# A decoder step bound by TensorE: the high and low parts of the activations start at 44 different pairs of places in 256-byte blocks, and one ring's low weights stand 192 bytes beyond the high ones instead of 64

## The chip, the cores and the metric

One core of a Trainium2 chip runs the whole program as one launch. The metric is device time in microseconds (us). The median of two runs of the kernel before is 2691.72 us (2691.7 and 2691.73).

## What is computed

A two-layer decoder step on 320 tokens (256 of a prompt and 64 of 8 sample sequences), model width 2048, all in float32:

```
layer 0: gated linear attention (w_in: 2048 x 6144, w_out: 2048 x 2048), norm, MLP, norm
layer 1: gMLP spatial gating   (w_in: 2048 x 4096, w_out: 2048 x 2048), norm, MLP, norm
MLP:     square(relu(x @ w1)) @ w2          w1: 2048 x 8192, w2: 8192 x 2048
norm:    layer_norm(alpha * x + sublayer(x))
```

Nearly all the arithmetic is in products of a 2048 x 2048 block of weights with the 320 tokens. There are 23 such blocks: three of the attention's w_in, one of its w_out, four of w1 and four of w2 in each MLP, two of the gMLP's w_in and one of its w_out.

## The kernel before, in words

Activations lie transposed: features on the 128 partitions, the 320 tokens along the free dimension, and 16 tiles `k` of 128 features after each other. Each float32 operand is split into a rounded part ("high", `fp32r`) and the rest ("low"). A product of the two is three matmuls, in `mm3`: low weights with high activations (L161), high weights with low activations (L162), high weights with high activations (L163). Each loads its own 128 x 128 weights and streams the 320 columns of one activation tile. In what follows, three such matmuls are called a **triplet**.

`gemm` goes over the output columns in groups of 256. `group` goes over four **quarters** `q` of the 16 feature tiles. For each quarter `unit` fetches a 128 x 4 x 256 block of raw weights (512 KB), ACT rounds it into `wh` (L144), DVE subtracts to make `wl` (L145), and TensorE runs 2 x 4 triplets with it: 24 matmuls. So a block of weights is 8 groups x 4 quarters x 8 triplets = 256 triplets, and the quarter changes every 8 triplets.

The split weights go into rings of four buffers for high and four for low. Ring "a" serves the whole program. Ring "b" is added in `second_half`, during the attention's `w_out`, and from there on units take ring a and ring b in turn. A group has an even number of units, so a given quarter always meets the same ring. `Ring.part` puts a gap of `LINE // 4` = 16 floats (64 bytes) between the high and the low buffers.

Where the tiles start, counted in bytes from the last multiple of 256 (a **place**):

| tile | place before |
|---|---|
| `wh`, both rings | 0 |
| `wl`, both rings | 64 |
| activations `x`, `o`, `y`, `h` (high and low), every feature tile | 128 |
| activations `dg` (see below), feature tile `k` | 8k (0 to 120) |

The feature tiles of width 320 are 1280 bytes apart, five times 256, so all of a tensor have one place. `bigtile` sets it with `start = LINE // 2`. The tensors `dg` are the unnormalised input of the first two groups of a product that follows a norm (`gemm_of`, three times in the program); they have two more columns (322), so their feature tiles are 1288 bytes apart and the place moves by 8 bytes from one to the next. This is called the **raw stage** below.

The pairs of tensors that the change touches are those made by `parts(out, "y")` in `gemm_of` and by `parts(h_in, "h")` in `mlp`. `y` is the normalised input of w1 (and of the gMLP's w_in, and in place of it later the input of the gMLP's w_out); `h` is the input of w2, made afresh for each of the eight w2 blocks.

Of the kernel before, what the change touches and what calls it, by code (L numbers as in the profile page):

```python
# [8 lines left out]
F32 = mybir.dt.float32  # L9
F32R = mybir.dt.float32r  # L10
# [5 lines left out]
P = 128  # L16
# [4 lines left out]
T = TP + DB * DS  # L21
# [9 lines left out]
UK = 4  # L31
UN = 256
NU = KT // UK
WARM = 9
LINE = 64
BIG = KT * T + LINE
# [8 lines left out]
class Ring:  # L45


    def __init__(self, pool, tag):
        self.pool, self.tag, self.gap = pool, tag, False

    def part(self, p, name):

        t = self.pool.tile([P, UK, UN], F32R, tag=p + self.tag, name=name)
        if not self.gap:
            self.pool.tile([P, LINE // 4], F32, tag="gap", name=name + "_gap", bufs=1)
            self.gap = True
        return t


class Side:  # L60
# [17 lines left out]
def step_kernel(ctx: ExitStack, tc: tile.TileContext, A):  # L78
# [3 lines left out]
    def nm(s):  # L82
        uid[0] += 1
        return f"{s}_{uid[0]}"
# [3 lines left out]
    big = ctx.enter_context(tc.tile_pool(name="big", bufs=1))  # L88
# [8 lines left out]
    turn = [0]  # L97
    banks = [0]
    units = [0]

    def mmtile(n=T):

        if mx is not None:
            banks[0] = (banks[0] + 1) % 6
        return (mx if banks[0] > 3 else mm).tile([P, n], F32, tag="mm", name=nm("mm"), padded_shape=[P, 512])
# [19 lines left out]
    def col(c):  # L125
        return vec[:, c : c + 1]
# [38 lines left out]
    def group(w, row0, cols, rh, rl, evict, side=None, width=T, before=None):  # L165

        ps = [mmtile(width) for _ in range(2 * len(cols))]
        for q in range(NU):
            if before is not None:
                before(q)  # L170
            for i, c in enumerate(cols):
                wh, wl = unit(w, row0, q, c, next_ring())
                for n in range(2):
                    for kk in range(UK):
                        k = q * UK + kk
                        mm3(ps[2 * i + n][:], wh, wl, kk, n, rh, rl, k, 0, width, k == 0, k == KT - 1)
                if side is not None:
                    side()
        for n in range(2 * len(cols)):
            evict(n, ps[n])  # L180
# [11 lines left out]
    lp = l2 = z = None  # L192
# [5 lines left out]
    def bigtile(tag, dt, name, width=T):  # L198

        t = (lp if tag == "b1" else big).tile([P, BIG], dt, tag=tag, name=nm(name))
        start = LINE // 2 if width == T else 0
        return t[:, start : start + KT * width].rearrange("p (k t) -> p k t", t=width)

    def parts(pair, name, width=T):
        return bigtile(pair + "0", F32R, name + "h", width), bigtile(pair + "1", F32R, name + "l", width)

    xh, xl = parts("a", "x")  # L210
    o_all = bigtile("b0", F32, "o_all")

    gst = ExitStack()
# [129 lines left out]
    class Head:  # L343


        def __init__(hd, h):
            hd.h = h
            hd.eb, hd.ei, hd.ee = {}, {}, {}
# [484 lines left out]
    def gemm(w, row0, col0, rh, rl, evict, quad=False, side=None, before=None, before_last=None):  # L833

        i = 0
        while i < D // UN:
            n2 = 2 if quad and i == 0 else 1
            group(w, row0, [col0 + (i + m) * UN for m in range(n2)], rh, rl,
                  lambda n, ps, i=i: evict(2 * i + n, ps), side, before=before if i == 0 else before_last if i == D // UN - 1 else None)
            i += n2  # L840

    def gemm_of(norm, out, w, col0, evict_raw, evict):

        yh, yl = parts(out, "y")
        norm.close()
        side = Side([lambda j=j: norm.apply(j, yh, yl) for j in range(KT)], 3 * NU)
        group(w, 0, (col0, col0 + UN), *norm.raw, evict_raw, side, width=TW)
        side.flush()
        for i in range(2, D // UN):
            group(w, 0, (col0 + i * UN,), yh, yl, lambda n, ps, i=i: evict(2 * i + n, ps))  # L850
        return yh, yl

    def residual_gemm(w, rh, rl, row0, scale, vg, vb, raw, quad=False, side=None, before=None, last=False):

        norm = None

        def evict(j, ps):
            nonlocal norm
            if j == 0:
                norm = Norm(z, vg, vb, raw, last)  # L860
            zj = z[:, j, :]
            if j < KT // 2:
                nc.vector.scalar_tensor_tensor(zj, zj, scale, ps[:], op0=ALU.mult, op1=ALU.add)
            else:
                nc.vector.tensor_add(zj, zj, ps[:])
            norm.add(j)
            if j == KT // 2 - 1:
                for i in range(KT // 2, KT):
                    zi = z[:, i, :]
                    nc.vector.scalar_tensor_tensor(zi, zi, scale, norm.c[:], op0=ALU.mult, op1=ALU.subtract)  # L870

        gemm(w, row0, 0, rh, rl, evict, quad, side, before)
        return norm

    def mlp(i, norm, y_in, h_in, vg, vb, raw, last=False):

        w1, w2 = A["mlp_w1"][i], A["mlp_w2"][i]
        NC_ = 4
        for c in range(NC_):
            hs = []  # L880

            def sq_relu(j, x, r):
                if not hs:
                    hs.extend(parts(h_in, "h"))
                hh, hl = hs
                f = l2.tile([P, T], F32, tag="f", name=nm("f"))
                nc.vector.scalar_tensor_tensor(f[:], x, 0.0, r[:], op0=ALU.max, op1=ALU.mult)
                nc.scalar.copy(hh[:, j, 0:T], f[:])
                nc.vector.tensor_sub(hl[:, j, 0:T], f[:], hh[:, j, 0:T].bitcast(F32))

            def evict(j, ps):
                r = l2.tile([P, T], F32, tag="r", name=nm("r"))
                nc.scalar.activation(r[:], ps[:], AF.Relu)
                sq_relu(j, ps[:], r)

            def evict_raw(j, ps):
                t, wb_ = norm.correct(ps)
                r = l2.tile([P, T], F32, tag="r", name=nm("r"))
                nc.scalar.activation(r[:], t[:], AF.Relu, bias=wb_)
                sq_relu(j, r[:], r)  # L900

            if c == 0:
                yh, yl = gemm_of(norm, y_in, w1, 0, evict_raw, evict)
            else:
                gemm(w1, 0, c * D, yh, yl, evict)
            if c < NC_ - 1:
                def evz(j, ps, s=ALPHA if c == 0 else 1.0):
                    nc.vector.scalar_tensor_tensor(z[:, j, :], z[:, j, :], s, ps[:], op0=ALU.mult, op1=ALU.add)
                gemm(w2, c * D, 0, *hs, evz)
            else:  # L910
                return residual_gemm(w2, *hs, c * D, 1.0, vg, vb, raw, last=last)
# [35 lines left out]
    def put_v(j, x, bias):  # L947
        nonlocal v, nv
        if j == 0:
            v = bigtile("a0", F32, "v")  # L950
            nv = Norm(v, V_SG, V_SBB)
        vj = v[:, j, 0:T]
        nc.scalar.activation(vj, x, AF.Gelu, bias=bias)
        if j >= KT // 2:
            nc.vector.tensor_sub(vj, vj, nv.c[:])
        nv.add(j)
        if j == 3:
            spatial()

    def ev_v_raw(j, ps):  # L960
# [3 lines left out]
        put_v(j, t[:], bias[:])  # L964

    yh, yl = gemm_of(norm, "b", A["sg_w_in"], D, ev_v_raw, lambda j, ps: put_v(j, ps[:], col(V_SB + KT + j)))

    nv.close()
# [105 lines left out]
    for j in range(KT):  # L1074
        y, g, b = z[:, j, :], col(norm.vg + j), col(norm.vb + j)
# [78 lines left out]
```

## Time and profile before

| | |
|---|---|
| median of the runs | 2691.72 us |
| the profiled execution: first to last instruction | 2689.4 us |
| around it (median less span) | 2.3 us |
| TensorE (PE) busy | 2680.7 us, 100% of the span |
| weight loads (PEld) busy | 2658.8 us, 99% |
| DVE, ACT busy | 1550.3 us (58%), 1162.5 us (43%) |
| granted TensorE clock | 1.000 |

The profiled execution's time by the runs' measure is its span and the 2.3 us around it. "PE" rows are matmuls and "PEld" rows weight loads, which run beside them. Matmuls are pipelined: the time of one in a row (some 300 ns) is from its start to its modelled end, while the next starts after about 145 ns. What counts for the time is the distance from one start to the next, called the **pitch** below, which a timeline shows, or a row that gives the first start, the last start and the number of matmuls between.

### The profile page before, as it was taken

Reading aid. Unit: us, or ns where it says so; the run is one execution under the profiler, and the core shown is the slowest. Engines: PE = TensorE matmul, PEld = TensorE weight load, DVE = VectorE, ACT = ScalarE, POOL = GpSimd, SP = SyncE. Lnnn points to the kernel's source line nnn. Section 1 sums busy time; section 2 is a strip of 40 time slices with the busy share of each in tenths; the row PEclk is TensorE's granted clock in tenths of the full one; section 3 lists DMA queues with packets and bytes.
Section 4 is the critical chain, followed back from the end, with each engine's and each line's share of the span. In section 5 each row is a group of like instructions: output and inputs, shape, how many; then the busy total and the mean of one; then the engine's idle time right before and its main releaser. Section 6 shows DMA issues by size and latency. Waiting matters only on the chain.

```text
span 2689.4 us, 44906 instructions
## 1 busy us (share of the span) xinstructions
PE 2680.7 (100%) x18395; PEld 2658.8 (99%) x18395; DVE 1550.3 (58%) x2322; ACT 1162.5 (43%) x1638; POOL 226.4 (8%) x391
## 2 busy tenths in 40 slices
PE   9999999999999999999999999999999999999999
PEld 9999999999999999999999999999999999999998
DVE  7677677885444444444478776686444444444446
ACT  5455455564334334333446554355334333333434
POOL 4353341000000000000001032000000000000000
PEclk9999999999999999999999999999999999999999
DMA  8667667545445545444445555455445444454552
GB/s 252 220 196 249 217 198 253 189 142 159 155 150 155 151 150 156 150 153 152 150 152 161 157 158 149 134 165 153 153 150 156 150 152 154 150 155 150 152 154 79
DMA packets 138494, 442.42 MB, mean 165 GB/s; under 512 B 20912, under 2 KB 27952, under 8 KB 138288
## 3 DMA queue, kind: packets, MB, share of 16 engines
q1 hardware_dynamic: 121440, 408.08, 49.2%
q0 software_dynamic: 16304, 30.82, 3.7%
q8 instruction: 144, 2.36, 0.4%
q10 hardware_dynamic: 544, 0.66, 0.1%
q14 instruction: 62, 0.51, 0.1%
HBM read 409.60 MB, written 22.02 MB: 160 GB/s over the span
## 4 chain that ended last, share of the span: by engine, by line
PE 99%; DMA 0%; ACT 0%; DVE 0%; ACTq 0%; issue 0%; DVEq 0%
PE mm L161 32%; PE mm L163 32%; PE mm L162 31%; PE gl L631 1%; PE gl L634 1%; PE gl L589 1%; PE gl L1003 0%; PE gl L573 0%; DMA raw<-gla_w_in 0%; ACT z L1087 0%; DMA xr<-xT 0%; PE gl L558 0%; PE gl L603 0%; PE gl L574 0%; PE gl L552 0%; PE gl L1004 0%
## 5 line engine op out<-in xcount | busy, mean ns | idle before, releaser
L145 DVE TENSOR_TENSOR wl<-raw,wh 128x1024 fp32r<-128x1024 f32 (+1 forms) x740 | 902.3, 1220 | 953.2 <-ACT wh L144 950.9
L144 ACT CAST wh<-raw 128x1024 fp32r<-128x1024 f32 (+1 forms) x740 | 771.5, 1044 | 1251.9 <-PE mm L163 1127.1
L163 PE MATMUL mm<-yh,wh 128*128 128x320 f32 x2624 | 805.9, 307 | 0.0
L161 PE MATMUL mm<-yh,wl 128*128 128x320 f32 x2624 | 803.2, 309 | 0.0
L162 PE MATMUL mm<-yl,wh 128*128 128x320 f32 x2624 | 794.9, 303 | 0.0
L161 PE MATMUL mm<-hh,wl 128*128 128x320 f32 x2048 | 631.5, 308 | 0.0
L163 PE MATMUL mm<-hh,wh 128*128 128x320 f32 x2048 | 629.0, 307 | 0.0
L162 PE MATMUL mm<-hl,wh 128*128 128x320 f32 x2048 | 619.9, 303 | 0.0
L162 PEld LDWEIGHTS mm<-yl,wh 128*128 128x128 f32 x2624 | 492.7, 188 | 0.0
L163 PEld LDWEIGHTS mm<-yh,wh 128*128 128x128 f32 x2624 | 491.4, 187 | 0.0
L161 PEld LDWEIGHTS mm<-yh,wl 128*128 128x128 f32 x2624 | 491.0, 188 | 0.0
L161 PEld LDWEIGHTS mm<-hh,wl 128*128 128x128 f32 x2048 | 384.6, 188 | 0.0
L162 PEld LDWEIGHTS mm<-hl,wh 128*128 128x128 f32 x2048 | 384.6, 188 | 0.0
L163 PEld LDWEIGHTS mm<-hh,wh 128*128 128x128 f32 x2048 | 383.4, 187 | 0.0
L161 PE MATMUL mm<-xh,wl 128*128 128x320 f32 x768 | 238.2, 311 | 1.4 <-DVE wl L145 0.7
L163 PE MATMUL mm<-xh,wh 128*128 128x320 f32 x768 | 236.4, 309 | 0.0
L162 PE MATMUL mm<-xl,wh 128*128 128x320 f32 x768 | 235.2, 306 | 0.0
L161 PEld LDWEIGHTS mm<-xh,wl 128*128 128x128 f32 x768 | 144.1, 188 | 5.4 <-DVE wl L145 1.0
L162 PEld LDWEIGHTS mm<-xl,wh 128*128 128x128 f32 x768 | 144.3, 188 | 4.4 <-issue 1.2
L163 PEld LDWEIGHTS mm<-xh,wh 128*128 128x128 f32 x768 | 143.7, 187 | 2.6 <-issue 0.7
L1053 POOL CAST ident_r<-ident 128x128 fp32r<-128x128 f32 x1 | 0.3, 286 | 1027.9 <-PE gl L772 1027.9
L936 POOL DMA_DIRECT2D bsp<-sg_wT x1 | 0.6, 558 | 999.7 <-PE mm L163 999.7
(265 smaller groups left out, 2380.3 us busy)
## 6 DMA issues: line engine op xcount, KB each, us to landing
raw<-mlp_w SPq DMA_DIRECT2D x512, 512.0 KB, 3.5
raw<-gla_w_in SPq DMA_DIRECT2D x94, 512.0 KB, 4.1
raw<-sg_w_in SPq DMA_DIRECT2D x64, 512.0 KB, 3.6
st<-state SPq DMA_DIRECT2D x32, 512.0 KB, 5.7
o_state_s<-st POOLq DMA_DIRECT2D x32, 512.0 KB, 4.2
raw<-gla_w_out SPq DMA_DIRECT2D x32, 512.0 KB, 4.5
raw<-sg_w_out SPq DMA_DIRECT2D x32, 512.0 KB, 3.5
va<-blk POOLq DMA_DIRECT2D x128, 32.0 KB, 4.3
```

The source lines that it names most:

```text
L144: nc.scalar.copy(hi[:, ks, :], raw[:, ks, :])
L145: nc.vector.tensor_sub(lo[:, ks, :], raw[:, ks, :], hi[:, ks, :].bitcast(F32))
L161: nc.tensor.matmul(ps, wl[:, kk, s], x_h, start=first, stop=False)
L162: nc.tensor.matmul(ps, wh[:, kk, s], x_l, start=False, stop=False)
L163: nc.tensor.matmul(ps, wh[:, kk, s], x_h, start=False, stop=last)
L589: nc.tensor.matmul(pairs(pu), hd.ktp[:, kt, blk, :], hd.v_prompt(blk), start=(blk == 0), stop=(blk == 1))
L631: nc.tensor.matmul(po[:], qm[:, kt, b * P : (b + 1) * P], part[:], start=False, stop=(b == DB - 1 and kt == 1 and part is sth))
L634: nc.tensor.matmul(pairs(pu), kz[:, i, kt, g, :], hd.v_sample(g), start=True, stop=True)
L936: nc.gpsimd.dma_start(wsT, A["sg_wT"])
L1053: nc.gpsimd.tensor_copy(ident_r[:], ident[:])
```

## The change

A class `Act` takes the place of the plain tile for `y` and `h`. It puts each quarter (four feature tiles) at a place of its own, a multiple of 32 bytes given by a table, for the high and the low tensor apart. The quarters stand in the tile in the order of their places, so that they don't overlap; the tile has 256 bytes to spare, as before. The three `y` pairs and the eight `h` pairs with four quarters each make 44 pairs of places (high, low), all different; the pair (4, 4), which is the old 128 and 128, isn't among them. In ring b the gap between high and low weights becomes `3 * LINE // 4` = 48 floats, so its `wl` stands at place 192 instead of 64. Ring a stays.

```
 class Ring:
         self.pool, self.tag, self.gap = pool, tag, False
+        self.apart = LINE // 4 if tag == "a" else 3 * LINE // 4
...
-            self.pool.tile([P, LINE // 4], F32, tag="gap", name=name + "_gap", bufs=1)
+            self.pool.tile([P, self.apart], F32, tag="gap", name=name + "_gap", bufs=1)
...
+class Act:
+    def __init__(self, tile, places):
+        order = sorted(range(NU), key=lambda q: places[q])
+        self.tile = tile
+        self.start = [order.index(q) * UK * T + LINE // 8 * places[q] for q in range(NU)]
+
+    def __getitem__(self, at):
+        p, k, c = at
+        s = self.start[k // UK] + k % UK * T
+        return self.tile[p, s + (c.start or 0) : s + c.stop]
+
+H_PLACES = [
+    ((1, 4, 0, 5), (4, 1, 4, 4)), ((4, 6, 2, 3), (0, 4, 4, 4)), ...
+]
+Y_PLACES = [((4, 1, 6, 0), (7, 3, 0, 7)), ((4, 1, 7, 5), (5, 2, 7, 3)), ((1, 6, 3, 0), (6, 6, 3, 6))]
...
+    def placed(pair, name, places):
+        tiles = []
+        for i in range(2):
+            pool = lp if pair + str(i) == "b1" else big
+            tiles.append(Act(pool.tile([P, BIG], F32R, tag=pair + str(i), name=nm(name + "hl"[i])), places[i]))
+        return tiles
...
-        yh, yl = parts(out, "y")
+        yh, yl = placed(out, "y", Y_PLACES[gemms[0]])
...
-                    hs.extend(parts(h_in, "h"))
+                    hs.extend(placed(h_in, "h", H_PLACES[4 * i + c]))
```

In the built program every engine has the same instructions as before, in the same order and with the same waits; every tile has the same size and buffer. What differs is the address at which `y`, `h` and ring b's `wl` are written and read.

More of the change, by code (lines that the diff above doesn't have):

```diff
@@ L54, in part @@
         if not self.gap:
-            self.pool.tile([P, LINE // 4], F32, tag="gap", name=name + "_gap", bufs=1)
+            self.pool.tile([P, self.apart], F32, tag="gap", name=name + "_gap", bufs=1)
             self.gap = True
         return t
+class Act:
[8 more added lines that the diff above has]
+H_PLACES = [
+    ((1, 4, 0, 5), (4, 1, 4, 4)), ((4, 6, 2, 3), (0, 4, 4, 4)), ((1, 0, 4, 7), (0, 0, 2, 4)), ((1, 1, 5, 2), (1, 5, 1, 0)),
+    ((5, 5, 0, 3), (5, 0, 5, 1)), ((3, 2, 6, 7), (5, 6, 2, 3)), ((4, 4, 6, 7), (3, 6, 5, 0)), ((1, 0, 2, 3), (7, 3, 2, 7)),
+]
+Y_PLACES = [((4, 1, 6, 0), (7, 3, 0, 7)), ((4, 1, 7, 5), (5, 2, 7, 3)), ((1, 6, 3, 0), (6, 6, 3, 6))]
 class Side:
@@ L99, in step_kernel @@
     units = [0]
+    gemms = [0]
     def mmtile(n=T):
@@ L842, in gemm_of @@
     def gemm_of(norm, out, w, col0, evict_raw, evict):
-        yh, yl = parts(out, "y")
+        yh, yl = placed(out, "y", Y_PLACES[gemms[0]])
+        gemms[0] += 1
         norm.close()
```

## The prediction

> **What bounds the kernel now.** I read the page's busy times first, then its chain that ended last, then the groups of matmuls.
>
> ```profile
> span 2689.4 us, 44906 instructions
> ...
> PE 2680.7 (100%) x18395; PEld 2658.8 (99%) x18395; DVE 1550.3 (58%) x2322; ACT 1162.5 (43%) x1638; POOL 226.4 (8%) x391
> ...
> PE 99%; DMA 0%; ACT 0%; DVE 0%; ACTq 0%; issue 0%; DVEq 0%
> ...
> L145 DVE TENSOR_TENSOR wl<-raw,wh 128x1024 fp32r<-128x1024 f32 (+1 forms) x740 | 902.3, 1220 | 953.2 <-ACT wh L144 950.9
> L163 PE MATMUL mm<-yh,wh 128*128 128x320 f32 x2624 | 805.9, 307 | 0.0
> L161 PE MATMUL mm<-yh,wl 128*128 128x320 f32 x2624 | 803.2, 309 | 0.0
> L162 PE MATMUL mm<-yl,wh 128*128 128x320 f32 x2624 | 794.9, 303 | 0.0
> L161 PE MATMUL mm<-hh,wl 128*128 128x320 f32 x2048 | 631.5, 308 | 0.0
> L163 PE MATMUL mm<-hh,wh 128*128 128x320 f32 x2048 | 629.0, 307 | 0.0
> L162 PE MATMUL mm<-hl,wh 128*128 128x320 f32 x2048 | 619.9, 303 | 0.0
> ```
>
> PE is never idle: the chain is 99% PE, and the idle time before the matmuls of `y` and `h` is 0.0. So the kernel's time is the number of matmuls times their pitch, and nothing but the pitch can move it. The last six rows say how many triplets read the moved tensors: 2624 with `y` and 2048 with `h`, together **4672**. One nanosecond more in each triplet is 4.7 us of the kernel.
>
> Now the pitch. The row of L161 in a stretch of 100 us gives the first start, the last start and the count.
>
> ```profile
> L161 PE MATMUL mm<-yh,wl x232: 307/308/309, 999.8 to 1099.9; 128*128 128x320 f32 x116
> ```
>
> There are 231 triplets in 100.1 us: **433.3 ns** for a triplet, all with activations at place 128, high weights at 0 and low weights at 64. All the 100 us are alike: the durations lie within 307 to 309.
>
> Is this pitch a property of the matmuls, or can the places move it? Two things in the trace speak to that. The first is a timeline of the attention stage, behind another kind of matmul (L634), at the same places:
>
> ```profile
> 238.76 0.40 PE L634 MATMUL gl<-va,kz 128*128 128x512 f32 x1
> 239.00 0.31 PE L161 MATMUL mm<-xh,wl 128*128 128x320 f32 x1
> 239.15 0.31 PE L162 MATMUL mm<-xl,wh 128*128 128x320 f32 x1
> 239.29 0.31 PE L163 MATMUL mm<-xh,wh 128*128 128x320 f32 x1
> 239.44 0.31 PE L161 MATMUL mm<-xh,wl 128*128 128x320 f32 x1
> ...
> 239.88 0.31 PE L161 MATMUL mm<-xh,wl 128*128 128x320 f32 x1
> ...
> 241.61 0.31 PE L161 MATMUL mm<-xh,wl 128*128 128x320 f32 x1
> ```
>
> The first triplet takes 440 ns (239.00 to 239.44), the second 440, and the next four together 1.73 us, 432.5 each. The matmuls are the same, the addresses have the same places; only what ran before differs. So a disturbed sequence is some 7 ns slower per triplet, and it settles after two. The second is the raw stage, whose places differ from one feature tile to the next:
>
> ```profile
> 545.16 0.30 PE L161 MATMUL mm<-dgh,wl 128*128 128x322 f32 x1
> ...
> 552.24 0.31 PE L161 MATMUL mm<-dgh,wl 128*128 128x322 f32 x1
> ...
> L161 PE MATMUL mm<-dgh,wl x17: 304/309/315, 545.2 to 552.2; 128*128 128x322 f32 x17
> ```
>
> ```profile
> 559.89 0.31 PE L161 MATMUL mm<-dgh,wl 128*128 128x322 f32 x1
> ...
> 574.12 0.31 PE L161 MATMUL mm<-yh,wl 128*128 128x320 f32 x1
> ...
> L161 PE MATMUL mm<-dgh,wl x32: 308/310/317, 559.9 to 573.7; 128*128 128x322 f32 x32
> ```
>
> These are 16 triplets in 7.08 us (442.5 ns, places 0 to 24) and 32 in 14.23 us (444.7 ns, places 64 to 120), 444.0 on average. Two columns of 322 are extra: at 433.3 / 960 = 0.45 ns a column they cost 2.7 ns a triplet. What is left, 441.3, is **8.0 ns above** the settled triplet at place 128, and the durations spread over 304 to 317 where they were 307 to 309. The trace thus has two levels: 433.3 where places stay and the sequence has settled, about 441 where it is disturbed or the places change.
>
> **The change part by part.**
>
> *The places of `y` and `h`.* No instruction is added or removed, so the term is 4672 triplets times a difference of pitch. The trace has no settled stretch at another place, so I bound it. In the changed kernel the place is constant for the 8 triplets of a unit, and then the next quarter has another.
>
> - Lower bound of the likely cases: every pair settles to the same 433.3, but it has to settle anew in each unit. By the timeline that is two triplets of eight at about +7: 2 / 8 x 7 = 1.75 ns per triplet, or 4672 x 1.75 = 8 us.
> - Upper bound of the likely cases: the new pairs never do better than the raw stage, +8.0 ns on every triplet, or 4672 x 8.0 = 37 us.
>
> The rows nearest to the new stage lie on both sides: like the raw stage it goes through many places, like `y` and `h` before it stays long enough at one to settle. I take the middle, (1.75 + 8.0) / 2 = 4.9 ns a triplet, **+23 us**.
>
> *Ring b's low weights at 192.* This touches every unit of ring b from the attention's `w_out` on, half of the units. Inside `y` and `h` it is one more place among those that the bounds above cover, and I add nothing. Outside, in the raw stage (192 triplets) and most of `w_out`'s 256, at most half of the 448 triplets meet ring b. At the 8 ns of the raw stage either way that is 224 x 8.0 = 1.8 us up or down; I take nothing, since the raw stage's rows show no side.
>
> *The writers.* ACT and DVE write `y`, `h` and `wl` at other addresses. I cost this at nothing, because PE hides it:
>
> ```profile
> ACT wh L144 <- PE mm L163: 1127.1, 514, 3.8
> DVE wl L145 <- ACT wh L144: 950.9, 564, 4.2
> ```
>
> ACT waits 1127 us in all for PE to free a weight buffer, and DVE then waits for ACT. A unit's `wl` takes 1220 ns and its matmuls 8 x 433 ns = 3.5 us. Even a `wl` twice as long would be 2.4 us of 3.5, with the buffers of two rings ahead of PE. If that cover failed, an uncovered 1.2 us on each of the 292 units (4672 / 8 = 584, half in ring b) would be 350 us; nothing in the rows points there.
>
> *Sum.* The profiled execution's own time is 2689.4 + 2.3 = 2691.7 us, the same as the median of the runs. 2691.7 + 23 = **2715 us**, 0.9% above.
>
> A rule speaks against any effect. In the Trainium skill, "TensorE: Matmul & The Clock Gate", section "Step-by-step: what each phase is for", PE has two independent read ports into SBUF, and loading the next weights takes no read bandwidth from the running matmul; by that rule the place of either operand could not matter. The trace doesn't agree that matmuls of one size have one pitch (440 against 432.5 ns above), though it doesn't show which resource they share. The same page, section "Wait — 56ns, not 53.3ns?", gives N / 2.4 + 2.5 ns back to back, for 320 columns 135.8 ns or 407.5 ns a triplet: an estimate by which up to 25.8 ns a triplet (121 us) could be there to win, and the sum above would be nearer to a gain. The settled 433.3 ns lies far from it at the one pair measured, and the raw stage, over many places, doesn't come nearer.
>
> **The rivals.**
>
> - *Places don't matter, only disturbance does, and that is brief.* The matmuls settle within a triplet or at once, since the units follow without a gap. For it: the rows of `y` and `h`, which stand in different buffers, have the same 307 to 309 and 303. Against it: the raw stage runs without a gap and never settles. Time: 2692, up to the 8 us above, 2700. It is also the case in which the change does nothing that the time can show. The rule of two independent ports named above would give this case, too.
> - *Faster: other pairs settle lower.* L162's mean duration is 303 ns where L161 has 309 and L163 307, for the same shape: at the old places two of three matmuls are held longer than the third. If new pairs let all three run as L162 does, a triplet loses 6 + 4 = 10 ns, 4672 x 10 = 47 us, and the time is 2645; half of the pairs give 2668. For it: the ends 304 in the raw stage. Against: its median stands at 309 and 310, so most places are not better.
> - *Slower by over 2%: a bad phase that holds.* In the raw stage a bad place lasts one triplet, here it lasts a unit, and a sequence can settle into the long pattern as it settled into the short one at 128. Price: the raw stage's longest L161 has 317 where the median is 309 or 310, 7 to 8 ns in one matmul of the three, on top of the 8.0 ns: 16 ns a triplet, 75 us, 2767. It decides the verdict from 54 / 4672 = 11.5 ns a triplet. For it: the spread 304 to 317. Against: it needs nearly all pairs to be bad, and 44 different ones average out.
>
> **How the numbers follow.** Forecast, 2700 to 2735: 0.62. Places don't matter, 2688 to 2700: 0.17. Faster, 2645 to 2688: 0.12. The bad phase, 2735 to 2770: 0.09. About 2% (54 us) is what a measurement of this kernel can tell from no change. The range goes from 2670, which keeps the half of the faster case in which up to half of the pairs gain, to 2745, which takes in the raw stage's full price and a little more; outside are about 0.05 below and 0.08 above. Faster by over 2% needs below 2638, beyond the whole of that rival: 0.02. Slower by over 2%, above 2746: 0.08. Within 2%: 0.90.
>
> **What the profile after would show.** The start of the first raw stage stays at 545.2 us to about 1 us, since all before it keeps its places but for ring b in `w_out`. The pitch of L161 in stretches of `h` and `y` differs from quarter to quarter, each with its own level between about 425 and 450 ns, and its mean is near 438. L162's mean duration rises above 303 towards 306, since it has most to lose, and L161's and L163's stay near 308. PE stays at 100% and the chain at 99% PE; L145 stays at about 1.22 us. Wrong would be: the same pitch in all quarters (then places don't matter), a mean over 445 or under 430, or idle time before the matmuls, which no part of this reckons with.

## The result and the profile after

| | before | after |
|---|---|---|
| median of the runs | 2691.72 us | 2727.2 us (2727.04 and 2727.37) |
| span of the profiled execution | 2689.4 us | 2725.3 us |
| ratio | | 1.0132, interval 1.0103 to 1.0162 |

The changed kernel is 35.5 us slower, 1.3%: clear of noise, and less than 2%. Line numbers moved: L161, L162 and L163 are L184, L185 and L186 now. From the page after, the busy times, the chain and the groups of matmuls (out<-in, count, busy us, mean ns of one, idle before):

```profile
span 2725.3 us, 44906 instructions
...
PE 2716.9 (100%) x18395; PEld 2694.6 (99%) x18395; DVE 1553.2 (57%) x2322; ACT 1163.2 (43%) x1638; POOL 226.6 (8%) x391
...
PE 99%; DMA 0%; ACT 0%; DVE 0%; ACTq 0%; issue 0%; DVEq 0%
...
L168 DVE TENSOR_TENSOR wl<-raw,wh 128x1024 fp32r<-128x1024 f32 (+1 forms) x740 | 901.1, 1219 | 979.9 <-ACT wh L167 977.7
L167 ACT CAST wh<-raw 128x1024 fp32r<-128x1024 f32 (+1 forms) x740 | 771.8, 1044 | 1284.7 <-PE mm L186 1158.9
L186 PE MATMUL mm<-yh,wh 128*128 128x320 f32 x2624 | 811.9, 310 | 0.0
L185 PE MATMUL mm<-yl,wh 128*128 128x320 f32 x2624 | 810.8, 309 | 0.0
L184 PE MATMUL mm<-yh,wl 128*128 128x320 f32 x2624 | 804.3, 309 | 0.0
L186 PE MATMUL mm<-hh,wh 128*128 128x320 f32 x2048 | 633.7, 309 | 0.0
L184 PE MATMUL mm<-hh,wl 128*128 128x320 f32 x2048 | 632.9, 309 | 0.0
L185 PE MATMUL mm<-hl,wh 128*128 128x320 f32 x2048 | 632.4, 309 | 0.0
```

PE is still busy all the time, DVE and ACT do the same work in the same time (1219 and 1044 ns) and only wait longer for PE. The three matmuls of a triplet were 309, 303 and 307 ns long; now all stand at 309 or 310. The row of one line over one product with `h`, before and after, gives the pitch:

```profile
L161 PE MATMUL mm<-hh,wl x255: 307/308/309, 657.9 to 768.0; 128*128 128x320 f32 x128
...
L184 PE MATMUL mm<-hh,wl x256: 305/308/315, 659.7 to 772.2; 128*128 128x320 f32 x128
```

After, 255 triplets take 112.5 us, 441 ns each; before, 254 take 110.1 us, 433 ns each. Over the triplets of `y` and `h` that take between 400 and 500 ns (4571 of the 4672; most of the rest are interrupted by other matmuls), from the starts in both traces, the means are 441.0 after and 433.4 before. 7.6 ns times 4672 is 35.5 us, nearly the whole 35.9 us by which the two spans differ. Counted from the starts, 35.0 us of it arise between the first triplet of `y` and the last of `h`, and 1.0 us before that, nearly all in `w_out`, where ring b is already in use. The first raw stage starts that much later, at 546.14 instead of 545.16:

```profile
546.14 0.31 PE L184 MATMUL mm<-dgh,wl 128*128 128x322 f32 x1
```

A timeline of the third use of `y` in the first MLP shows how it comes about. These are the starts of L184, one for each triplet; from 1002.24 on one unit with the pair (1, 3), from 1005.76 on the next with (6, 0):

```profile
1002.24 0.31 PE L184 MATMUL mm<-yh,wl 128*128 128x320 f32 x1
...
1002.68 0.31 PE L184 MATMUL mm<-yh,wl 128*128 128x320 f32 x1
...
1003.12 0.31 PE L184 MATMUL mm<-yh,wl 128*128 128x320 f32 x1
...
1003.56 0.31 PE L184 MATMUL mm<-yh,wl 128*128 128x320 f32 x1
...
1005.76 0.31 PE L184 MATMUL mm<-yh,wl 128*128 128x320 f32 x1
...
1006.21 0.31 PE L184 MATMUL mm<-yh,wl 128*128 128x320 f32 x1
...
1006.65 0.31 PE L184 MATMUL mm<-yh,wl 128*128 128x320 f32 x1
...
1007.10 0.31 PE L184 MATMUL mm<-yh,wl 128*128 128x320 f32 x1
...
1007.53 0.31 PE L184 MATMUL mm<-yh,wl 128*128 128x320 f32 x1
```

The first unit takes 440 ns a triplet from end to end (3.52 us for eight). The second goes up and down, 450, 440, 450, 430 by the rows' 10 ns; over all its repetitions 449 and 438 alternate. So these sequences do settle within a unit, but not at 433.

### The profile page after: what moved, and what is told of

Its sections match the earlier page's. It is cut to its first block, busy times and chain, and to the rows that moved or that the text cites. A ratio compares the mean times of both kernels' runs of the same rounds, so it can differ in the third digit from the quotient of the medians.

```text
span 2725.3 us, 44906 instructions
## 1 busy us (share of the span) xinstructions
PE 2716.9 (100%) x18395; PEld 2694.6 (99%) x18395; DVE 1553.2 (57%) x2322; ACT 1163.2 (43%) x1638; POOL 226.6 (8%) x391
## 4 chain that ended last, share of the span: by engine, by line
PE 99%; DMA 0%; ACT 0%; DVE 0%; ACTq 0%; issue 0%; DVEq 0%
PE mm L184 32%; PE mm L186 32%; PE mm L185 32%; PE gl L661 1%; PE gl L664 1%; PE gl L619 1%; PE gl L1034 0%; PE gl L603 0%; DMA raw<-gla_w_in 0%; ACT z L1118 0%; DMA xr<-xT 0%; PE gl L588 0%; PE gl L633 0%; PE gl L604 0%; PE gl L582 0%; PE gl L1035 0%
## 5 line engine op out<-in xcount | busy, mean ns | idle before, releaser
L168 DVE TENSOR_TENSOR wl<-raw,wh 128x1024 fp32r<-128x1024 f32 (+1 forms) x740 | 901.1, 1219 | 979.9 <-ACT wh L167 977.7
L167 ACT CAST wh<-raw 128x1024 fp32r<-128x1024 f32 (+1 forms) x740 | 771.8, 1044 | 1284.7 <-PE mm L186 1158.9
L186 PE MATMUL mm<-yh,wh 128*128 128x320 f32 x2624 | 811.9, 310 | 0.0
L185 PE MATMUL mm<-yl,wh 128*128 128x320 f32 x2624 | 810.8, 309 | 0.0
L184 PE MATMUL mm<-yh,wl 128*128 128x320 f32 x2624 | 804.3, 309 | 0.0
L186 PE MATMUL mm<-hh,wh 128*128 128x320 f32 x2048 | 633.7, 309 | 0.0
L184 PE MATMUL mm<-hh,wl 128*128 128x320 f32 x2048 | 632.9, 309 | 0.0
L185 PE MATMUL mm<-hl,wh 128*128 128x320 f32 x2048 | 632.4, 309 | 0.0
L185 PEld LDWEIGHTS mm<-yl,wh 128*128 128x128 f32 x2624 | 493.5, 188 | 0.0
L186 PEld LDWEIGHTS mm<-yh,wh 128*128 128x128 f32 x2624 | 493.2, 188 | 0.0
L184 PEld LDWEIGHTS mm<-yh,wl 128*128 128x128 f32 x2624 | 491.5, 188 | 0.0
L185 PEld LDWEIGHTS mm<-hl,wh 128*128 128x128 f32 x2048 | 385.0, 188 | 0.0
L184 PEld LDWEIGHTS mm<-hh,wl 128*128 128x128 f32 x2048 | 384.9, 188 | 0.0
L186 PEld LDWEIGHTS mm<-hh,wh 128*128 128x128 f32 x2048 | 384.8, 188 | 0.0
L184 PE MATMUL mm<-xh,wl 128*128 128x320 f32 x768 | 237.9, 311 | 1.2 <-ACT xh L260 1.0
L186 PE MATMUL mm<-xh,wh 128*128 128x320 f32 x768 | 236.3, 309 | 0.0
L185 PE MATMUL mm<-xl,wh 128*128 128x320 f32 x768 | 235.2, 306 | 0.0
L184 PEld LDWEIGHTS mm<-xh,wl 128*128 128x128 f32 x768 | 144.0, 188 | 5.2 <-ACT xh L260 1.2
L185 PEld LDWEIGHTS mm<-xl,wh 128*128 128x128 f32 x768 | 144.2, 188 | 4.6 <-issue 1.2
L186 PEld LDWEIGHTS mm<-xh,wh 128*128 128x128 f32 x768 | 143.6, 187 | 2.6 <-issue 0.7
```

The source lines that it names most:

```text
L167: nc.scalar.copy(hi[:, ks, :], raw[:, ks, :])
L168: nc.vector.tensor_sub(lo[:, ks, :], raw[:, ks, :], hi[:, ks, :].bitcast(F32))
L184: nc.tensor.matmul(ps, wl[:, kk, s], x_h, start=first, stop=False)
L185: nc.tensor.matmul(ps, wh[:, kk, s], x_l, start=False, stop=False)
L186: nc.tensor.matmul(ps, wh[:, kk, s], x_h, start=False, stop=last)
```

## Experiments

In all of them "level" means the mean triplet of a pair of places, from start to start. A level that is settled is taken from the fourth to the seventh triplet of a unit. Two theories are told apart first. **Patterns**: every combination of places settles into a repeating pattern with a level of its own, and 433 belongs to the old one. **Disturbance**: every place settles at 433, and each change of place costs a few unsettled triplets.

**e1: the places alone.** Ring b's low weights back at 64; the tables stay.

```
-        self.apart = LINE // 4 if tag == "a" else 3 * LINE // 4
+        self.apart = LINE // 4
```

> The places of y and h as in the changed kernel, ring b's low weights back at 64. Patterns (every combination of places settles into a repeating pattern of its own length, and the short one of 433 ns belongs to activations at 128 with low weights at 64): the triplets of y and h stay at 440 to 442 on average, 4672 x 7.5 = 35 us above before, 2724 to 2728. Disturbance (each change of place costs a few unsettled triplets, every place settles at 433): also near 2727, with the loss in the first two triplets of each unit. Ring b (its 192 makes the loss): at most 2700.

2722.45 us, ratio 1.0115 (1.0099 to 1.013): 31 us above before. The mean triplet is 440.2. The settled levels lie between 433 and 450, with 20 of 44 at 440. The first two triplets of a unit have 439.6 and 441.1 on average, the other six 439.0 to 441.1: the loss isn't at the start of the units, so disturbance does not explain these 31 us; the 192 bytes are not the main part either.

**e2: ring b's 192 bytes alone.** Both tables hold nothing but place 4.

```
-H_PLACES = [ ((1, 4, 0, 5), (4, 1, 4, 4)), ...
+H_PLACES = [ ((4, 4, 4, 4), (4, 4, 4, 4)), ...
+Y_PLACES = [ ((4, 4, 4, 4), (4, 4, 4, 4)), ...
```

> All activations at place 128, as before; only ring b's low weights stand at 192. Patterns: ring b's units go to 440, ring a's stay at 433 to 436, half of 5000 triplets x 6.7 ns plus a little, 2706 to 2716. Disturbance: the low weights' place changes with every unit, two of eight triplets at +7, 2699 to 2702, in both rings alike. Ring b: the whole 35 us, 2725 or more.

2713.41 us, ratio 1.0081 (1.0064 to 1.0098): 22 us. By ring, ring b's triplets went to 440.3 and ring a's to 435.7. In ring a the eight triplets of a unit run 440, 437, 439, 433, 433, 433, 433, 435 on average: it comes back to the short level after three. The starts of L190 over one unit of ring a show it, 440, 440, 440, 430, 430, 440, 430, 430 by the rows' 10 ns:

```profile
669.91 0.31 PE L190 MATMUL mm<-hh,wl 128*128 128x320 f32 x1
...
670.35 0.31 PE L190 MATMUL mm<-hh,wl 128*128 128x320 f32 x1
...
670.79 0.31 PE L190 MATMUL mm<-hh,wl 128*128 128x320 f32 x1
...
671.23 0.31 PE L190 MATMUL mm<-hh,wl 128*128 128x320 f32 x1
...
671.66 0.31 PE L190 MATMUL mm<-hh,wl 128*128 128x320 f32 x1
...
672.09 0.31 PE L190 MATMUL mm<-hh,wl 128*128 128x320 f32 x1
...
672.53 0.31 PE L190 MATMUL mm<-hh,wl 128*128 128x320 f32 x1
...
672.96 0.31 PE L190 MATMUL mm<-hh,wl 128*128 128x320 f32 x1
...
673.39 0.31 PE L190 MATMUL mm<-hh,wl 128*128 128x320 f32 x1
```

The patterns' figures hold. Disturbance exists beside them: ring a, at its old places, loses 2.3 ns a triplet because each of its units follows one of ring b. 22 and 31 us add up to 53, and both together cost 35.5: each part alone takes most of the triplets that it touches from 433 to 440, and the other finds nothing more to take from those.

**e3: constant places.** One pair for a whole product, 64 bytes in both rings.

```
+H_PLACES = [ ((0, 0, 0, 0), (0, 0, 0, 0)), ((1, 1, 1, 1), (1, 1, 1, 1)), ... ((7, 7, 7, 7), (7, 7, 7, 7)), ]
+Y_PLACES = [((4, 4, 4, 4), (4, 4, 4, 4)), ((4, 4, 4, 4), (0, 0, 0, 0)), ((0, 0, 0, 0), (4, 4, 4, 4))]
```

> Low weights at 64 in both rings, and one pair of places for all quarters of a product: the eight h pairs at (p, p), p = 0 to 7; the y pairs at (4, 4), (4, 0) and (0, 4). So no place changes within a product. Patterns: 433 in the h pair (4, 4) and the first y, 440 or more in most others; 3456 triplets x about 7 ns = 24 us, 2710 to 2720. Disturbance: every product at 433 to 434, 2692 to 2695.

2714.83 us, ratio 1.0086 (1.0066 to 1.0106). Rows of the line of low weights, here L190, over the products at (0, 0), (2, 2), (3, 3) and (4, 4):

```profile
L190 PE MATMUL mm<-hh,wl x255: 307/310/310, 657.7 to 769.5; 128*128 128x320 f32 x128
L190 PE MATMUL mm<-hh,wl x255: 307/308/310, 1104.9 to 1215.5; 128*128 128x320 f32 x128
L190 PE MATMUL mm<-hh,wl x256: 307/308/313, 1326.9 to 1440.1; 128*128 128x320 f32 x128
L190 PE MATMUL mm<-hh,wl x254: 308/308/308, 1908.0 to 2017.6; 128*128 128x320 f32 x127
```

254 triplets in 111.8 us are 440.2; 254 in 110.6 are 435.4; 255 in 113.2 are 443.9; 253 in 109.6 are 433.2. (5, 5) and (6, 6) have 440.0, (7, 7) 441.7, (1, 1) 440.0. Among the `y` products, (4, 4) has 433.4, (4, 0) 440.1 and (0, 4) 441.3. So no place changes within a product, and still only (4, 4) runs at 433. This decides between the two theories: each combination of places has a level of its own, and of these ten only the old one has 433.

What ACT and DVE write meanwhile doesn't set the level. In the trace before, the 1830 triplets during which DVE is busy over 90% of the time take 433.5 ns on average, and the 1917 during which it is busy under 10% take 433.3; for ACT it is 433.6 (1048 triplets) and 433.4 (2273).

**e4: everything moved by 96 bytes.** In the kernel before:

```
-    cp.tile([P, LINE - 8], F32, tag="fill", name="fill")
+    cp.tile([P, LINE - 8 + 24], F32, tag="fill", name="fill")
```

> The kernel before, with every tile behind the constants moved by 96 bytes: activations at place 224, high weights at 96, low weights at 160, all distances as before. If the distances between the streams make the pattern: 433 everywhere, 2691 to 2693. If the place in the 256-byte block itself does: 440 in most triplets, 2715 to 2730.

2691.5 us, ratio 1.000 (0.9989 to 1.001). The old pattern returns row for row, 308 for L161 and 303 for L162:

```profile
L161 PE MATMUL mm<-hh,wl x249: 308/308/308, 660.1 to 767.6; 128*128 128x320 f32 x125
L162 PE MATMUL mm<-hl,wh x250: 302/303/303, 659.8 to 767.7; 128*128 128x320 f32 x125
```

Under this shift, then, what counts is how activations and weights stand to each other, not where they stand in the block; other shifts were not run.

**e5, e6, e7: other gaps and the remaining pairs.** These look for a version that beats both kernels. They change the tables, the gap of each ring and the fill behind, so that the high weights keep their places (e5: 0 bytes in ring a, 128 in ring b; e6: 32 and 96; e7: 64 in both, with the pairs not yet seen and steps of 8 and 16 bytes). The edit of the gap in e5, in floats:

```
-        self.apart = LINE // 4 if tag == "a" else 3 * LINE // 4
+        self.apart = 0 if tag == "a" else 32
```

> Low weights at the place of the high ones (gap 0) in ring a, 128 bytes beyond in ring b, and y and h at 44 other pairs, 16 of them with high and low alike in steps of 16 bytes. With gap 0 and like places each matmul has the same distance to the weights that are loaded beside it. Distances with steps (a matmul waits a whole number of 6.67 ns steps, most often two, which gives 146.7 ns and 440 a triplet): levels of 433, 440 and 447 and means between them, on average 438 to 442, 2710 to 2730 us; some distances with one step only, 140 ns a matmul and down to 420 a triplet, would show a faster version. No steps: pitches spread evenly, with no level preferred.

> Low weights 32 bytes beyond the high ones in ring a, 96 in ring b, and y and h at 22 pairs with each. Distances with steps: again mostly 440, average 438 to 442, 2710 to 2730 us, a few at 433. If the gap of 64 were special: no pair at 433 here, average 441 or more.

> Low weights at 64 in both rings; y and h at the 19 pairs of 32-byte places that no run has shown yet and at 25 others, most of them 8 or 16 bytes beside the old pair. Distances with steps: the pairs 8 bytes beside the old one stay at 433 if a step has room, those 16 beside go to 440 or not; average 437 to 441, 2705 to 2725 us. If 433 is the least that this stream can do: no pair below 433.

2724.46 us (ratio 1.0124, 1.0094 to 1.0153), 2730.89 (1.0148, 1.0118 to 1.0177) and 2722.68 (1.0117, 1.0088 to 1.0146). With after, e1 and e3, 195 combinations of gap and two places have now been seen. Their settled levels:

```
433.3 (within 0.6)   10 combinations         65 x 6.667
440.0 (within 0.6)   some 90 combinations    66 x 6.667
all                  433.0 to 452.9          mean 440.2
```

Besides the old one, 433 belongs for example to (0, 5) and (6, 5) with 64 bytes, (0, 0) and (4, 4) with 128, (2, 2) with 32. The levels in between are patterns over two or more triplets, such as 431 and 442 in turn, at (1, 1) with 128. The gap of 64 isn't special. With gap 0 and like places for high and low, 14 of 16 distances in steps of 16 bytes have a settled level within 0.6 of 440.0. **No combination is below 433** (the 433.0 is a pattern of 438, 432 and 430, 433.3 over its three triplets), so none of these beats the kernel before; the 420 that e5 held possible was not found.

**e8: 448 columns instead of 320.** At the old places:

```
+        wide = isinstance(rh, Act)
+        width = WIDE if wide else width          # WIDE = 448
...
+        if c.stop == WIDE and k >= KT // 2:
+            s -= WIDE - T
```

> All places as in the kernel before, but each matmul of y and h streams 448 columns instead of 320: 128 columns of a neighbouring feature tile come with it, and their results are left unused or, in the second half of the feature tiles, take the tokens' place. The moved start is a multiple of 256 bytes, so the distances stay. If the waits belong to the weight load that runs beside the stream: the triplet grows by the columns alone, 3 x 128 at 0.42 ns (the trace before has 0.23 us for 512 columns and 0.147 for 320), about 160 ns to 593 ns, and the time by 4672 x 0.16 us = 748 to 3440 us. If they come with the columns streamed: 433.3 x 1.4 = 607 ns and 3500 us.

3500.75 us, ratio 1.3007 (1.2969 to 1.3045). The row of low weights (L193) in a product with `h`:

```profile
L193 PE MATMUL mm<-hh,wl x254: 363/363/363, 691.8 to 845.3; 128*128 128x448 f32 x127
```

253 triplets in 153.5 us: 606.7 ns, which is 1.4 times 433.3. The theory that the waits belong to the weight load beside the stream gave 593 and does not hold at this pair; e10 shows that one pair is not enough to decide it.

**e9 and e12: 64 and 8 weights instead of 128**, in all but the first and last feature tile.

```
+        if isinstance(rh, Act) and not first and not last:
+            s, ps = slice(n * P, n * P + P // 2), ps[0 : P // 2, :]       # e12: 8 for P // 2
```

> All places as in the kernel before, but the matmuls of y and h load only 64 of the 128 weights, except in the first and the last feature tile: half of the output features get two of sixteen tiles' sums only. The columns streamed are the same. If a wait comes with each 256 bytes of weights read beside the stream: one wait instead of two in most matmuls, a triplet of 413 to 420, 4672 x 7/8 x 13 to 20 ns less, 2610 to 2640 us. If the waits come with the streamed columns or once per matmul whatever it loads: 433, 2690 us.

> All places as before, but the matmuls of y and h load only 8 of the 128 weights, except in the first and last feature tile; most output features lack fourteen of sixteen tiles' sums. If the weight load that runs beside the stream makes the waits, 4088 triplets fall to 400 to 413 ns: 2555 to 2610 us. If the stream has them by itself: 433 to 440, 2690 to 2715 us.

2708.76 us (ratio 1.0064, 1.0041 to 1.0087) and 2716.38 us (1.0094, 1.0064 to 1.0123): slower than before, although less is loaded. First the weight loads of e9 and e12 (busy us, mean ns), then their rows of L192 in a product with `h`:

```profile
L192 PEld LDWEIGHTS mm<-yh,wl 128*64 128x64 f32 x2296 | 306.9, 134 | 23.6
...
L192 PEld LDWEIGHTS mm<-yh,wl 128*8 128x8 f32 x2296 | 202.2, 88 | 119.6
```

```profile
L192 PE MATMUL mm<-hh,wl x254: 304/308/314, 658.8 to 769.4; 128*64 128x320 f32 x112, 128*128 128x320 f32 x15
...
L192 PE MATMUL mm<-hh,wl x254: 304/309/310, 659.7 to 770.8; 128*8 128x320 f32 x112, 128*128 128x320 f32 x15
```

The loads fall from 188 to 134 and 88 ns, and the triplets go from 433 to 437 (253 in 110.6 us) and 439 (253 in 111.1). The length of the load changes which pattern comes out, but the triplet does not get shorter with it. (With fewer weights the results also go to fewer partitions, so the two change together.)

**e11: 64 columns five times.** At the old places, the stream goes over the first 64 columns of a tile, 256 bytes, five times. They begin at place 128, so they are halves of two blocks, and each pass goes through the same places as the next 64 columns would.

```
+            x_h, x_l = (x[:, 0:LINE].unsqueeze(1).to_broadcast([P, T // LINE, LINE]) for x in (x_h, x_l))
+            ps = ps.rearrange("p (a b) -> p a b", b=LINE)
```

> All places as before, but each matmul of y and h streams the first 64 columns of its tile five times over instead of 320 columns: it stays in 256 bytes and most tokens get another token's sums. If the waits come from walking on through the blocks, the triplet falls towards 3 x 320 columns at 0.417 to 0.43 ns, 400 to 413 ns, and the time by 95 to 155 us to 2535 to 2600. If they come with the rate of reading, wherever it reads: 433 to 440, 2690 to 2725 us.

2691.49 us, ratio 1.0001 (0.999 to 1.0012); in a product with `h` (L193):

```profile
L193 PE MATMUL mm<-hh,wl x253: 308/308/308, 658.9 to 768.1; 128*128 128x320 f32 x127
```

252 triplets in 109.2 us: 433.3, the old pattern. Whether the stream walks on to further blocks or reads the same bytes again makes no difference to the time.

**e10: e3's pairs with 448 columns.** The edits of e3 and e8 together (the start is moved back where it lies in the second half of the tile).

> The constant pairs of e3 (h at (p, p), y at (4, 4), (4, 0) and (0, 4), low weights at 64) with 448 columns streamed for 320 as in e8, the additional results unused or in the tokens' place. If the waits are a share of the columns streamed, the pairs with 440 ns for 320 columns have 1.4 x 440 = 616 ns, (3, 3) 620, and the old pair 607: about 3530 us. If a pair costs a fixed step per triplet on top of a share, they have 613 ns: 3524 us.

3505.19 us, ratio 1.3025 (1.2987 to 1.3063), less than either reading gave. Products at (0, 0), (5, 5), (4, 4) and (0, 4), L193:

```profile
L193 PE MATMUL mm<-hh,wl x255: 362/367/368, 691.8 to 847.6; 128*128 128x448 f32 x128
L193 PE MATMUL mm<-hh,wl x252: 367/367/367, 2711.2 to 2865.2; 128*128 128x448 f32 x126
L193 PE MATMUL mm<-hh,wl x256: 363/363/368, 2399.8 to 2554.5; 128*128 128x448 f32 x128
L193 PE MATMUL mm<-yh,wl x255: 362/362/369, 3176.1 to 3328.6; 128*128 128x448 f32 x128
```

613.4, 613.5, 606.7 and 600.4 ns. Of the seven like pairs beside (4, 4), five have the 613 of the second reading, and (6, 6) and (7, 7) have 610. The time falls short of it above all by (0, 4), with 960 triplets at 600, and by (4, 0) at 608. With 320 columns (0, 4) was worse than (4, 4), 441.3 against 433.4; with 448 it is better. From 320 to 448 columns (0, 4) grows by 159 ns, (4, 4) by 173 and (2, 2), from 435.5 to 613.3, by 178. So a pair's level neither scales with the columns nor carries a fixed surcharge for all pairs: which pair is good depends on the width of the matmul. The 159 of (0, 4) is what the theory of the weight load gave in e8, so that theory is not refuted for every pair.

## Why the prediction was right, point by point

- **What bounds the kernel: right.** PE stays at 100%, the chain at 99%, and 4672 triplets times the difference of their pitch is all of the 35.5 us but for about 1 us in `w_out`.
- **The term of the places: its size was off.** I took 4.9 ns a triplet, the middle of 1.75 and 8.0; it measured 7.6, 35.5 us instead of 23. The step that failed is the lower bound. It said that every pair settles to the same 433.3 and pays only for two triplets at the start of a unit. e3 shows that pairs settle, but mostly at 440. The cost of disturbance itself was read rightly from the triplets behind L634: e2's ring a pays it, 2.3 ns a triplet where the bound said 1.75. But it comes on top only of a pair whose own level is 433. The upper bound, the raw stage's 8.0 ns, was nearly the result. That the middle came within range is partly luck: half of it was a case that the changed kernel doesn't have. Why the raw stage, where the place moves with every triplet, costs about as much as the mean of many settled pairs was not examined.
- **Ring b: right as part of the same bounds, but not small by itself.** Alone it costs 22 us (e2). That it adds only about 5 to e1's 31, 1 of them in `w_out`, is what "one more place among those" meant. Nothing was added for `w_out` and the raw stage, with 1.8 us up or down as the bound: `w_out` came out 1 us longer, and the three raw stages, from their first start to the first of `y`, kept their 28.96 us to 0.02 us each.
- **The writers: right.** L168 has 1219 ns where L145 had 1220, and PE's idle time before the matmuls of `y` and `h` stays at 0.0.
- **What the profile would show.** L162's duration was to rise from 303 towards 306; it rose to 309, L163's by 2 to 3, L161's hardly, so the loss stands where it was expected but is larger. Levels between 425 and 450 were expected for the quarters, with a mean near 438; they lie between 436 and 449, with a mean of 441. The first raw stage was to start at 545.2 us to about 1 us; it starts at 546.1.
- **The rivals.** "Places don't matter" falls with e3. "Other pairs settle lower" falls on 195 combinations with 320 columns: none is below 433. With 448 columns one of ten pairs, (0, 4), does lie below the old one. "A bad phase that holds" exists, 449 at (6, 4), but 44 pairs average out, as its counterargument said.
- **The rule of two independent read ports**, from the Trainium skill, "TensorE: Matmul & The Clock Gate", section "Step-by-step: what each phase is for": e9 and e12 agree with it in that a smaller load frees nothing for the stream. That the places then make no difference, as I read it, does not follow: they make 35.5 us here, and in e2 a new place of the loaded weights alone takes the triplet from 433 to 440. The estimate of 407.5 ns a triplet from the same page's figure was reached by no combination; the least is 433.

What stays open is what the stream waits for. Shown is that the places of activations against weights set the level of a triplet (e1 to e7). At the old pair it does not depend on walking on through the blocks (e11) and does not fall with fewer weights to load (e9, e12); how it grows with the columns streamed differs from pair to pair (e8, e10). The place of the results in PSUM and a stream without any loads beside it were not tried.

## What to carry to other kernels

Where PE is busy all the time, the pitch between starts is the number to watch; busy shares and the durations of 303 to 310 ns hardly show a loss of 1.3%. Where tiles start against each other can be worth that much, so after any change of tile sizes, pads or pools compare the pitch of the main matmuls with the best one known, and look again when the width of the matmul changes. A settled stretch at one place says nothing of another place; a stretch of the same program that happens to go through many places (here the raw stage, 8.0 ns against 7.6) can come nearer to the price.

## What was unexpected of the hardware

- Settled triplets prefer steps of 6.67 ns: 433.3, 440.0, 446.7 for 320 columns, 600, 606.7 and 613.3 for 448. About half of 195 combinations settle within 0.6 ns of 433.3 or 440.0.
- Loading 8 weights instead of 128 beside the same stream makes it slower at the old places, 439 ns against 433 a triplet.
- Five passes over 64 columns cost what 320 different columns cost, 433.3 ns a triplet.
